# One probability tile for both key blocks, a first piece fed by kinds of parts, and last norms on ScalarE, in a hybrid decoder layer

## The chip, the core and the metric

The kernel runs on one core of one Trainium2 chip. Five engines work in parallel and meet through semaphores: TensorE (PE in the profile; its weight loads are listed apart as PEld), VectorE (DVE), ScalarE (ACT), GpSimd (POOL) and SyncE (SP), which here only issues transfers. Operands lie in SBUF, matmul results in PSUM, inputs and outputs in DRAM. The metric is the device time of one execution in microseconds; lower is better. Before the change it is 973.95, the median of three runs.

## What is computed

One layer over 1024 tokens with 16 learned tokens in front, width 1024, all in float32. Normalised input is projected once into queries, keys, values and two inputs of a recurrence. Eight attention heads (64 wide, two key/value heads) look at a window of 128 keys and at a per-head sink; a gated recurrence with a short convolution runs beside them. Both go through an output projection and a norm onto the residual stream; a feed-forward of width 4096 with squared relu follows.

```python
u = RMSNorm(h)
z = u @ W_in -> [q | k | v | x_rec | y_rec]
...
h += RMSNorm(concat(B_out, A_out) @ W_out)
h += RMSNorm(W2 relu(W1 RMSNorm(h))^2)
...
kk = jnp.concatenate([jnp.pad(kb, blk_pad)[:, :-1], kb], axis=2)
s = jnp.einsum("bnqkgd,bnskd->bnkgqs", qb, kk,
               preferred_element_type=jnp.float32) * scale
...
valid = (diff >= 0) & (diff < WINDOW) & (kpos[:, None, :] >= PAD)
s = jnp.where(valid[None, :, None, None], s, NEG)
m = jnp.maximum(jnp.max(s, axis=-1, keepdims=True), sink)
p = jnp.exp(s - m)
denom = jnp.sum(p, axis=-1, keepdims=True) + jnp.exp(sink - m)
o = jnp.einsum("bnkgqs,bnskd->bnqkgd", (p / denom).astype(v.dtype), vv)
```

Window and block are both 128. So query i of a block may see key i' of its own block where i' <= i, and key i' of the block before where i' > i: of each pair of keys at the same place in the two blocks exactly one is valid.

## The kernel before

**Precision.** Each float32 operand of a large matmul is kept as two parts, a rounded high part and a low part (what the rounding left), and a product is three matmuls: high by high, high by low, low by high (`mm3`, lines 121 to 125). ACT writes the high part, DVE subtracts it from the source to get the low one (`split`, 93 to 100; `split_scaled`, 115).

**Order.** A scheduler lays out each engine's instructions in program order with priorities; `behind` (105) adds an order by hand between two instructions, `lut` (81) keeps ACT's table functions in their written order. Buffers are slots of named pools (`raw`, `ws`, `a`, `b`, `c`, `d`, `e`); a load into a slot waits for the slot's last reader. SP issues most loads, POOL the accumulating stores.

**Start.** x comes in tiles of 128 tokens, with the 16 learned tokens in front. `norm_rows` (197 to 203) squares a tile on ACT, takes the power -0.5 on POOL (`rstd_of`, 155 to 165) and scales on DVE (202). `transposed` (235 to 250) turns the tile by PE and splits it into the two parts of u. This goes by four pieces of tokens (272, 256, 256, 256). For each piece the loop at 345 projects K, V, the first Q pair and the first recurrence input. The weights' parts are made at 277 to 281, ahead of and after the first piece's transposes. `put_k` (300 to 305) writes the high part of K on ACT, its copy into the other half of the partitions on DVE (304) and the low part on DVE (305).

**Attention.** A unit is a pair j of heads (one from each key/value head, h = 0 and 1) and a half of the sequence (four query blocks): 8 units, 16 heads-and-halves. `scores` (432 to 484) makes 128 x 256 scores per query block (previous and own key block), adds the mask and takes the minimum of the negated scores in one DVE instruction (467), exponentiates on ACT, and scales by the reciprocal sum (480). `attend` (486 to 523) turns the probabilities by PE, eight 128 x 128 transposes per head (495), splits them and multiplies by V (506): a key block serves two query blocks, so its matmul is 256 wide, except the first and the last, which are 128. Masks for the general and the first block are made at 365 to 382, V's parts at 409 to 422. Between the units the matmuls of other projections and of the recurrence are put as fill (568 to 600).

**Middle and end.** The recurrence's gates are block-diagonal matrices, built in a zeroed tile (604). Output projection, norm and feed-forward follow. In the feed-forward's last part the four token tiles of the second half and then those of the first are closed one by one: `finish_early` (1120 to 1128), `finish_half` (1132 to 1146), `finish_late` (1148 to 1180). `finish_late` adds both column halves' results, sums squares (1165), takes the power -0.5 on POOL (1173) and combines (1177) with the residual, which was either loaded before or is added by an accumulating store of POOL. `LASTW` (1041) names the slot pools of the last weights.

Of the kernel before, what the change touches and what calls it, by code (L numbers as in the profile page):

```python
# [16 lines left out]
P = 128  # L17
# [20 lines left out]
def hybrid_layer(  # L38
# [76 lines left out]
    def split_scaled(hi, lo, src, scale):  # L115
        nc.scalar.activation(hi, src, AF.Copy, scale=scale)
        nc.vector.scalar_tensor_tensor(
            lo, src, scale, f32(hi), op0=ALU.mult, op1=ALU.subtract
        )

    def mm3(dst, lhs, rhs, start, stop):
        (lh, ll), (rh, rl) = lhs, rhs
        nc.tensor.matmul(dst, lh, rh, start=start, stop=False, skip_group_check=True)  # L123
        nc.tensor.matmul(dst, lh, rl, start=False, stop=False, skip_group_check=True)  # L124
        nc.tensor.matmul(dst, ll, rh, start=False, stop=stop, skip_group_check=True)  # L125
# [29 lines left out]
    def rstd_of(ssq_parts, n=P):  # L155
# [8 lines left out]
        nc.gpsimd.tensor_tensor(rs[:n], ms[:n], half_pow[:n], op=ALU.pow)  # L164
# [32 lines left out]
    def norm_rows(src, n):  # L197
        xn = slot("d", [P, D])
        ssq = small.tile([P, 1], F32, name="ssq", tag="ssq")
        nc.scalar.activation(xn[:n], src, AF.Square, scale=RMS_SC, accum_out=ssq[:n])  # L200
        rs = rstd_of([ssq[:n]], n)
        nc.vector.tensor_scalar(xn[:n], src, rs, None, op0=ALU.mult)
        return xn
# [13 lines left out]

    ALL = [(0, 272), (272, 256), (528, 256), (784, 256)]
    REAL2 = [(16, 512), (528, 512)]

# [5 lines left out]
    nc.vector.tensor_copy(vm.rearrange("p a b -> p (a b)"), zero[:, :256])  # L226
# [8 lines left out]
    def transposed(b, xn):  # L235
        t0, n = ALL[b]
        for kc in range(KC):
# [3 lines left out]
            for s, m in xn:  # L241
                nc.tensor.transpose(
                    pt[:, o : o + m], s[:m, kc * P : (kc + 1) * P], ident[:m, :m]
                )
                o += m
            uh, ul = u[kc]
            split_scaled(
                uh[:, t0 : t0 + n], ul[:, t0 : t0 + n], pt[:, :n],
                g_mix_col[:, kc : kc + 1],
            )  # L250

# [25 lines left out]
    wk = split_w(rk, "b")  # L277
    wv = split_w(rv, "b")
    transposed(0, xn)
    wq = split_w(rq)  # L280
    wx = split_w(rx)
# [7 lines left out]


    khh = [slot("b", [P, T], F32R) for _ in range(2)]
    kl = [slot("b", [P, T], F32R) for _ in range(2)]

    vk = [slot("b", [P, 8, P], F32R) for _ in range(2)]
    HALF = (slice(0, HD), slice(HD, P))
    vt = slot("c", [P, TT])
    for h in range(2):
        nc.gpsimd.memset(f32(kl[h][HALF[1 - h]]), 0.0)

    def put_k(hh, lo, src):  # L300
        for h in range(2):
            r, o = HALF[h], HALF[1 - h]
            nc.scalar.copy(hh[h][r], src[r])
            nc.vector.tensor_copy(hh[h][o], src[r])
            nc.vector.tensor_tensor(lo[h][r], src[r], f32(hh[h][r]), op=ALU.subtract)  # L305

    def sink_k(acc, t0, n):
        o = 0
        if t0 == 0:
            m = slice(0, NMETA)  # L310
            put_k(
                [km[:, 0, m], km[:, 1, m]], [km[:, 2, m], km[:, 3, m]], acc[:, m]
            )
            o = NMETA
        c = slice(t0 + o - NMETA, t0 - NMETA + n)
        put_k(
            [khh[0][:, c], khh[1][:, c]], [kl[0][:, c], kl[1][:, c]], acc[:, o:]
        )

    def sink_v(acc, t0, n):  # L320
        nc.scalar.copy(vt[:, t0 : t0 + n], acc)

    def new_q():
# [3 lines left out]
        def sink_q(acc, t0, n):  # L327
            c = slice(t0 - NMETA, t0 - NMETA + n)
            for h in range(2):
                r, o = HALF[h], HALF[1 - h]  # L330
                split_scaled(q[h][r, c], q[h][o, c], acc[r], HD ** -0.5)
# [10 lines left out]

    q0, sink_q0 = new_q()
    xr0, sink_x0 = new_x("c")
    for b in range(4):
        if b:
            transposed(b, normed(b))
        piece = [ALL[b]]
        project(wk, piece, sink_k)
        project(wv, piece, sink_v)  # L350
        project(wq, piece if b else [(16, 256)], sink_q0)
        project(wx, piece, sink_x0)
# [4 lines left out]
    for c in range(NLRU):  # L357
# [7 lines left out]
    mask = const.tile([P, 256], F32, name="mask")  # L365
    nc.gpsimd.memset(mask, 0.0)
    nc.gpsimd.affine_select(
        out=mask[:, 0:P], in_=mask[:, 0:P], pattern=[[1, P]], compare_op=ALU.is_gt,
        fill=NEG, base=0, channel_multiplier=-1,
    )  # L370
    nc.gpsimd.affine_select(
        out=mask[:, P:256], in_=mask[:, P:256], pattern=[[-1, P]],
        compare_op=ALU.is_ge, fill=NEG, base=0, channel_multiplier=1,
    )
    mask1 = const.tile([P, 256], F32, name="mask1")
    nc.gpsimd.memset(mask1[:, 0:P], NEG)
    nc.gpsimd.memset(mask1[:, 0:NMETA], 0.0)
    nc.gpsimd.affine_select(
        out=mask1[:, 0:NMETA], in_=mask1[:, 0:NMETA], pattern=[[1, NMETA]],
        compare_op=ALU.is_gt, fill=NEG, base=P - NMETA, channel_multiplier=-1,  # L380
    )
    nc.gpsimd.tensor_copy(mask1[:, P:256], mask[:, P:256])
# [30 lines left out]

    pv = bank("o")
    nc.tensor.transpose(pv[:NMETA, :P], vt[:, :NMETA], ident)
    put_v([vm[:NMETA, 0, :], vm[:NMETA, 1, :]], pv[:NMETA, :P])
    for b in range(2):
# [4 lines left out]
        put_v([vk[0][:, 4 * b : 4 * b + 4, :], vk[1][:, 4 * b : 4 * b + 4, :]], pv)  # L422
# [9 lines left out]
    def scores(j, half, q):  # L432
        sn = [slot("c", [P, 4, 257]) for _ in range(2)]
# [3 lines left out]
        for h in range(2):  # L437
            nc.vector.tensor_copy(
                sn[h][:, :, 256], nsink[:, j + 4 * h : j + 4 * h + 1].to_broadcast([P, 4])
            )  # L440
        for bp in range(2):
            for h in range(2):
# [21 lines left out]
                for i in range(2):  # L464
                    b = 4 * half + 2 * bp + i
                    k = 2 * bp + i
                    nc.vector.tensor_tensor_reduce(
                        out=sn[h][:, k, 0:256], in0=sp_[:, i, :],
                        in1=mask1 if b == 0 else mask, scale=-1.0,
                        scalar=nsink[:, j + 4 * h : j + 4 * h + 1],  # L470
                        op0=ALU.add, op1=ALU.min, accum_out=negm[:, h, k : k + 1],
                    )
                    lut(
                        sn[h][:, k, :], sn[h][:, k, :], AF.Exp, scale=-1.0,
                        bias=negm[:, h, k : k + 1], accum_out=den[:, h, k : k + 1],
                    )
        for h in range(2):
            nc.vector.reciprocal(rden[:, h, :], den[:, h, :])
            for k in range(4):
                nc.vector.tensor_scalar(  # L480
                    sn[h][:, k, 0:256], sn[h][:, k, 0:256], rden[:, h, k : k + 1],
                    None, op0=ALU.mult,
                )
        return sn

    def attend(j, half, sn):
        flat = [t_.rearrange("p a b -> p (a b)") for t_ in sn]
        for h in range(2):
            ph, pl = pair("c", [P, 1024])
            for bp in range(2):  # L490
                pt = bank("pt")
                for i in range(2):
                    for s in range(2):
                        o = (2 * i + s) * P
                        nc.tensor.transpose(  # L495
                            pt[:, o : o + P],
                            sn[h][:, 2 * bp + i, s * P : (s + 1) * P], ident,
                        )
                c = slice(512 * bp, 512 * bp + 512)
                split(ph[:, c], pl[:, c], pt)  # L500
            po = bank("o")

            def av(kb, oc, n, pc, first, last):
                v = vm[:, h, :] if kb == 0 else vk[h][:, kb - 1, :]
                for k, p_ in enumerate((ph, pl)):
                    nc.tensor.matmul(  # L506
                        po[:, oc : oc + n], v, p_[:, pc : pc + n],
                        start=first and k == 0, stop=last and k == 1,
                        skip_group_check=True,
                    )  # L510

            kb0 = 4 * half
            av(kb0, 0, P, 0, True, False)
            for i in range(3):
                av(kb0 + 1 + i, i * P, 256, P + 256 * i, False, False)
            av(kb0 + 4, 3 * P, P, 7 * P, False, True)

            r, o = HALF[h], HALF[1 - h]
            part, whole = flat[h][r, 0:512], flat[0][r, 512:1024]
            nc.scalar.copy(part, po[o, :])  # L520
            nc.vector.tensor_tensor(whole, po[r, :], part, op=ALU.add)
        ah, al = at[half][j // 2]
        split(ah[:, j % 2, :], al[:, j % 2, :], flat[0][:, 512:1024])
# [80 lines left out]
    nc.gpsimd.memset(graw, 0.0)  # L604
# [411 lines left out]
    def product_by_parts(acc, w, op):  # L1016
# [25 lines left out]
        ("raw", None), ("e", "raw"), ("b", None), ("b", None), ("raw", "e"), ("b", None),  # L1042
# [43 lines left out]


# [32 lines left out]
    def finish_early(j):  # L1120
        acc = facc["1", j]
        o = slot("a", [P, D])
        ssq = [squares(o[:, c], acc[:, c], n) for n, c in enumerate(COLS)]
        nc.vector.scalar_tensor_tensor(
            o, acc, rstd_of(ssq), gffn_b, op0=ALU.mult, op1=ALU.mult
# [6 lines left out]
    def finish_half(j):  # L1132
# [6 lines left out]
        )  # L1139
        h = None  # L1140
        if j > 1:
            h = slot("d", [P, D])
            nc.sync.dma_start(h, out[j * P : (j + 1) * P, :])
            nc.gpsimd.tensor_scalar(ssq, ssq, EPS, None, op0=ALU.add)
# [137 lines left out]
```

## Time and profile before

| what | value |
| --- | --- |
| median of three runs | 973.95 us (972.76 to 975.39) |
| profiled execution, whole time | 972.95 us |
| its span in the profile | 971.1 us |
| outside the span | 1.85 us |
| mean granted TensorE clock | 0.999 |
| instructions | 12490 |
| first projection matmul starts | 11.18 us |
| 48 matmuls of K and V, first piece, end | 22.42 us |
| last matmul starts | 963.72 us |
| first raw weight load near the end, issue to landing | 907.68 to 916.87 us |

The profile is of one execution. A busy time is the sum over an engine's instructions; a share is of the span. Start to start distances of matmuls are read from the trace's timeline, since matmuls overlap and their ends are modelled. Masked reductions (L467) number 64 and take 0.41 us each, scalings of the probabilities (L480) 64 of 0.285, low parts of the turned probabilities 32 of 0.6.

### The profile page before, as it was taken

The numbers are of one execution on the slowest core, as the hardware profiler recorded it, in microseconds if no ns is written. First come the engines' busy times: TensorE is split into PE (matmuls) and PEld (weight loads), VectorE is DVE, ScalarE is ACT, GpSimd is POOL, SyncE is SP. The second block draws the span as 40 slices with busy tenths as digits, with TensorE's granted clock in tenths as the row PEclk, the third lists the DMA queues.
The fourth block names the chain that finished last, engine by engine and source line by source line (L and its number), as shares of the span: only waits on it lengthen the run. The fifth ranks groups of instructions, "written<-read, shape, count | busy, mean of one in ns | idle before, by whom it ended". The sixth has DMA issues, their size and how long they took to land.

```text
span 971.1 us, 12490 instructions
## 1 busy us (share of the span) xinstructions
PE 953.7 (98%) x4782; PEld 803.0 (83%) x4782; DVE 674.6 (69%) x997; ACT 502.0 (52%) x809; POOL 82.4 (8%) x109
## 2 busy tenths in 40 slices
PE   6999999999999999999999999999999999999997
PEld 6999999888878887888888878888888888888786
DVE  6679997775976686665645465468557676779694
ACT  6646673567844554343555556555433344445350
POOL 4100000000002100000000000000111000003152
PEclk9999999999999999999999999999999999999999
DMA  9002001012234466576522264323678765548923
GB/s 296 23 1 66 23 23 44 23 48 64 84 119 144 159 207 209 173 251 209 198 87 87 97 206 125 114 87 114 172 176 198 186 224 187 184 163 195 223 80 87
DMA packets 88219, 130.13 MB, mean 134 GB/s; under 512 B 13624, under 2 KB 52552, under 8 KB 88160
## 3 DMA queue, kind: packets, MB, share of 16 engines
q1 hardware_dynamic: 79792, 107.33, 33.4%
q0 software_dynamic: 7792, 20.45, 10.1%
q10 hardware_dynamic: 576, 1.57, 0.4%
q8 instruction: 37, 0.61, 0.2%
q14 instruction: 22, 0.18, 0.1%
HBM read 110.46 MB, written 18.87 MB: 133 GB/s over the span
## 4 chain that ended last, share of the span: by engine, by line
PE 89%; DVE 4%; DMA 3%; issue 2%; ACT 1%; POOL 0%; SPq 0%; POOLq 0%; DVEq 0%; ACTq 0%
PE ps_acc L124 11%; PE ps_acc L123 11%; PE ps_acc L125 11%; PE ps_s L125 6%; PE ps_pt L123 6%; PE ps_s L124 6%; PE ps_pt L125 6%; PE ps_s L123 6%; PE ps_pt L124 6%; PE ps_o L124 5%; PE ps_o L123 5%; PE ps_o L125 5%; PE ps_o L506 2%; PE ps_pt L495 1%; DMA raw<-in_w_ff_dram 1%
## 5 line engine op out<-in xcount | busy, mean ns | idle before, releaser
L95 ACT CAST ws<-raw 128x1024 fp32r<-128x1024 f32 (+1 forms) x69 | 70.7, 1024 | 126.6 <-PE ps_o L124 48.8
L98 DVE TENSOR_TENSOR ws<-raw,ws 128x1024 fp32r<-128x1024 f32 (+1 forms) x70 | 83.5, 1194 | 59.6 <-ACT ws L95 59.5
L123 PE MATMUL ps_acc<-a,ws 128*128 128x256 f32 (+2 forms) x272 | 90.5, 333 | 0.6 <-DVE b L305 0.6
L124 PE MATMUL ps_acc<-a,ws 128*128 128x256 f32 (+2 forms) x272 | 89.8, 330 | 0.0
L125 PE MATMUL ps_acc<-a,ws 128*128 128x256 f32 (+2 forms) x272 | 89.4, 329 | 0.0
L98 DVE TENSOR_TENSOR b<-b,b 128x1024 fp32r<-128x1024 f32 (+2 forms) x48 | 57.6, 1201 | 24.7 <-PE ps_o L124 17.1
L95 ACT CAST ws<-e 128x1024 fp32r<-128x1024 f32 x43 | 45.0, 1046 | 55.3 <-PE ps_o L124 28.1
L95 ACT CAST b<-b 128x1024 fp32r<-128x1024 f32 (+2 forms) x48 | 49.4, 1030 | 42.8 <-DVE b L788 40.0
L98 DVE TENSOR_TENSOR ws<-e,ws 128x1024 fp32r<-128x1024 f32 x43 | 52.6, 1222 | 21.6 <-ACT ws L95 21.6
L123 PEld LDWEIGHTS ps_acc<-a,ws 128*128 128x128 f32 x272 | 51.2, 188 | 4.9 <-DVE b L305 0.8
L125 PEld LDWEIGHTS ps_acc<-a,ws 128*128 128x128 f32 x272 | 51.2, 188 | 4.6
L124 PEld LDWEIGHTS ps_acc<-a,ws 128*128 128x128 f32 x272 | 51.2, 188 | 3.9
L164 POOL TENSOR_TENSOR rs<-ms,half_pow 128x1 f32<-128x1 f32 (+1 forms) x31 | 21.3, 692 | 356.5 <-DVE ms L160 355.1
L123 PE MATMUL ps_acc<-ws,b 128*128 128x512 f32 (+1 forms) x120 | 46.3, 386 | 0.4 <-ACT ws L95 0.4
L124 PE MATMUL ps_acc<-ws,b 128*128 128x512 f32 (+1 forms) x120 | 46.5, 388 | 0.2 <-DVE ws L98 0.2
L125 PE MATMUL ps_acc<-ws,b 128*128 128x512 f32 (+1 forms) x120 | 46.2, 385 | 0.0
L123 PE MATMUL ps_pt<-ws,b 128*128 128x512 f32 x112 | 44.1, 394 | 0.0
L124 PE MATMUL ps_pt<-ws,b 128*128 128x512 f32 x112 | 44.1, 394 | 0.0
L125 PE MATMUL ps_pt<-ws,b 128*128 128x512 f32 x112 | 44.0, 393 | 0.0
L123 PE MATMUL ps_s<-ws,b 128*128 128x512 f32 x110 | 43.4, 395 | 0.0
L124 PE MATMUL ps_s<-ws,b 128*128 128x512 f32 x110 | 43.3, 393 | 0.0
L125 PE MATMUL ps_s<-ws,b 128*128 128x512 f32 x110 | 43.3, 393 | 0.0
(381 smaller groups left out, 2690.1 us busy)
## 6 DMA issues: line engine op xcount, KB each, us to landing
raw<-in_w_ff_dram SPq DMA_DIRECT2D x62, 512.0 KB, 4.0
e<-in_w_ff_dram SPq DMA_DIRECT2D x45, 512.0 KB, 3.6
d<-in_w_ff_dram SPq DMA_DIRECT2D x12, 512.0 KB, 3.8
s_dram<-d POOLq DMA_DIRECT2D x12, 512.0 KB, 3.9
raw<-in_w_in_dram SPq DMA_DIRECT2D x9, 512.0 KB, 3.6
c<-in_x_dram SPq DMA_DIRECT2D x8, 512.0 KB, 8.5
d<-in_x_dram SPq DMA_DIRECT2D x8, 512.0 KB, 4.6
out_dram<-raw SPq DMA_DIRECT2D x8, 512.0 KB, 2.6
```

Source lines behind the costliest of these rows:

```text
L95: nc.scalar.copy(hi, src)
L98: low = nc.vector.tensor_tensor(lo, src, f32(hi), op=ALU.subtract).ins
L123: nc.tensor.matmul(dst, lh, rh, start=start, stop=False, skip_group_check=True)
L124: nc.tensor.matmul(dst, lh, rl, start=False, stop=False, skip_group_check=True)
L125: nc.tensor.matmul(dst, ll, rh, start=False, stop=stop, skip_group_check=True)
L164: nc.gpsimd.tensor_tensor(rs[:n], ms[:n], half_pow[:n], op=ALU.pow)
L495: nc.tensor.transpose(pt[:, o : o + P], sn[h][:, 2 * bp + i, s * P : (s + 1) * P], ident,)
L506: nc.tensor.matmul(po[:, oc : oc + n], v, p_[:, pc : pc + n], start=first and k == 0, stop=last and k == 1, skip_group_check=True,)
```

## The change

**Attention.** Scores of both key blocks go into one 128 x 128 tile per query block. The scores come out negated (q is scaled by a negative factor). ACT copies the own block's scores into the tile, DVE overwrites with the previous block's where the key lies above the diagonal (`above`); for the first block a second predicated copy fills the missing keys with a large number (`far`). One DVE reduction takes the minimum over 129 columns (128 and the sink), four exponentials and one normalisation follow, and four transposes per head in place of eight. After the split, POOL makes a second copy of each part in which only the own block's keys are kept and the rest is zero. The product with V is: all entries by V of the previous block, plus the masked copy by the difference of own and previous V. That makes 16 matmuls of 128 columns per head. POOL forms the differences (`vdf`), and V's parts are made from float32 copies in SBUF (`vf`, `vm_f`).

**First piece.** Only wk's high part is made ahead of the first transposes; ACT's and DVE's work is chained by hand; K's and V's matmuls of the first piece run by kinds: high by high for all eight chunks, then high by low, then low by high. The norms of the next two tiles stand between. POOL's clearing of the low parts of K moves to its start. K's copies in the other half of the partitions are made after the fourth piece by POOL transfers. Each later piece's transposes are ordered behind the matmuls of the piece before it; the clearing of `graw` (line 604) is ordered behind POOL's last power.

**Last norms.** The root is taken by ACT and inverted by DVE; ACT's table for it is loaded once ahead of the last part. The tile j = 2 takes the accumulating store as j = 0 and 1 do; j = 3 combines column half by column half. The first of the last weights has its buffer in `b` and not in `raw`.

Counts of instructions, before and after: PE 4782 and 4814 matmuls, DVE 947 and 831, ACT 658 and 673, POOL 107 and 141, SP 222 and 220.

```diff
+    def root_rstd(ssq, bias, n=P):
+        sd = small.tile([P, 1], F32, name="sd", tag="sd")
+        lut(sd[:n], ssq, AF.Sqrt, bias=bias)
+        rs = small.tile([P, 1], F32, name="rs", tag="rs")
+        nc.vector.reciprocal(rs[:n], sd[:n])
         return rs[:n]
...
+    def part(acc, w, piece, k, last=2):
+        t0, n = piece
+        for kc in range(KC):
+            last_mm[0] = nc.tensor.matmul(
+                acc[:, :n], w[k // 2][:, kc, :], u[kc][k % 2][:, t0 : t0 + n],
...
-    wk = split_w(rk, "b")
-    wv = split_w(rv, "b")
+    wk = high_w(rk, "b")
     transposed(0, xn)
-    wq = split_w(rq)
-    wx = split_w(rx)
+    low_w(wk, rk)
+    wv = high_w(rv, "b")
+    low_w(wv, rv)
+    wq = high_w(rq)
+    low_w(wq, rq)
...
-            nc.vector.tensor_copy(hh[h][o], src[r])
...
+            for a, w in zip(acc, (wk, wv)):
+                part(a, w, piece, 0)
+                part(a, w, piece, 1)
+            xn = [(norm_rows(xt[2], P, True), P)]
+            part(acc[0], wk, piece, 2)
+            sink_k(acc[0][:, : piece[1]], *piece)
...
+    for h in range(2):
+        r, o, m = HALF[h], HALF[1 - h], slice(P - NMETA, P)
+        nc.gpsimd.dma_start(f32(khh[h][o]), f32(khh[h][r]))
+        nc.gpsimd.dma_start(f32(km[o, h, m]), f32(km[r, h, m]))
...
-                for i in range(2):
-                    b = 4 * half + 2 * bp + i
-                    k = 2 * bp + i
-                    nc.vector.tensor_tensor_reduce(
-                        out=sn[h][:, k, 0:256], in0=sp_[:, i, :],
-                        in1=mask1 if b == 0 else mask, scale=-1.0,
...
+                s_ = sn[:, h, 2 * bp : 2 * bp + 2, 0:P]
+                nc.scalar.copy(s_, sp_[:, :, P:256])
+                nc.vector.copy_predicated(
+                    s_, above_i.rearrange("p (a b) -> p a b", a=1).to_broadcast([P, 2, P]),
+                    sp_[:, :, 0:P],
+                )
...
+            nc.vector.tensor_reduce(
+                negm[:, h, :], sn[:, h], axis=mybir.AxisListType.X, op=ALU.min
+            )
...
+            nc.vector.tensor_tensor(
+                sn[:, h, :, 0:P], sn[:, h, :, 0:P],
+                rden[:, h, :].to_broadcast([P, 4, P]), op=ALU.mult,
+            )
...
+            for i in range(4):
+                nc.tensor.transpose(pt[:, i * P : (i + 1) * P], sn[:, h, i, 0:P], ident)
+            pt = pt.rearrange("p (a b) -> p a b", a=4)
+            split(ph[:, 0], pl[:, 0], pt)
+            for p_ in (ph, pl):
+                nc.gpsimd.affine_select(
+                    out=p_[:, 1], in_=f32(p_[:, 0]), pattern=[[0, 4], [1, P]],
+                    compare_op=ALU.is_ge, fill=0.0, base=0, channel_multiplier=-1,
                 )
...
+            for s in range(2):
+                for i in range(4):
+                    b = 4 * half + i
+                    v = vd[h][:, b, :] if s else vk[h][:, b - 1, :] if b else vm[:, h, :]
+                    for k, p_ in enumerate((ph, pl)):
+                        nc.tensor.matmul(
+                            po[:, i * P : (i + 1) * P], v, p_[:, s, i, :],
...
-            av(kb0, 0, P, 0, True, False)
-            for i in range(3):
-                av(kb0 + 1 + i, i * P, 256, P + 256 * i, False, False)
-            av(kb0 + 4, 3 * P, P, 7 * P, False, True)
...
-    nc.gpsimd.memset(graw, 0.0)
+    behind(last_pow[0], nc.gpsimd.memset(graw, 0.0).ins)
...
-        ("raw", None), ("e", "raw"), ("b", None), ("b", None), ("raw", "e"), ("b", None),
+        ("b", None), ("e", "raw"), ("b", None), ("b", None), ("raw", "e"), ("b", None),
...
-            if j < 2:
+            if j < 3:
                 w_low[0] = nc.vector.scalar_tensor_tensor(
-                    o, acc, rstd_of([squares(o[:, c], acc[:, c], 0), ssq]), gffn_b,
+                    o, acc, root_rstd(squares(o[:, c], acc[:, c], 0), ssq), gffn_b,
...
+            if k == 1:
+                rs = root_rstd(ssq, 0.0)
+            w_low[0] = combine(o[:, c], acc[:, c], gffn_b[:, c], ALU.mult).name
...
-        nc.gpsimd.tensor_tensor(rs, ssq, half_pow, op=ALU.pow)
```

## The prediction, made before the changed kernel was run

> **What bounds the kernel now.** I read the totals first, then the chain that ended last, then both ends and two middle stretches by engine, then starts of single matmuls.
>
> ```profile
> span 971.1 us, 12490 instructions
> PE 953.7 (98%) x4782; PEld 803.0 (83%) x4782; DVE 674.6 (69%) x997; ACT 502.0 (52%) x809; POOL 82.4 (8%) x109
> PE 89%; DVE 4%; DMA 3%; issue 2%; ACT 1%; POOL 0%; SPq 0%; POOLq 0%; DVEq 0%; ACTq 0%
> ```
>
> PE is busy 98% of the span and holds 89% of the chain. So an edit pays only if it takes matmul time away, or shortens the two ends or one of PE's few stalls.
>
> ```profile
> 0.00:10.00 10.00, 2.68 (x14) 2.07 (x14) 4.61 (x9) 6.26 (x9) 6.36 (x22) 1.00 0.84 254
> 10.00:20.00 10.00, 9.32 (x42) 8.67 (x43) 8.61 (x14) 8.76 (x17) 3.65 (x7) 1.00 1.05 379
> 80.00:100.00 20.00, 20.00 (x147) 18.81 (x147) 19.65 (x54) 14.63 (x36) 0.00 (x0) 1.00 0.09 27
> 260.00:275.00 15.00, 14.59 (x64) 11.50 (x63) 15.00 (x16) 9.33 (x14) 0.00 (x0) 1.00 0.17 64
> 940.00:971.10 31.10, 24.00 (x132) 20.46 (x130) 18.33 (x28) 3.84 (x7) 11.87 (x7) 0.95 0.29 68
> ```
>
> Columns: stretch, length, busy time of PE, weight loads, DVE, ACT, POOL (counts), granted clock, DMA share, GB/s. PE lacks 7.3 us in the first ten, about 7 at the end (the last matmul starts at 963.72), and 0.4 in the stretch with the stall at 271.82. At 80 to 100 DVE is nearly full, yet PE never waits. Matmul starts after 20 us show four more gaps: 28.09 (0.79, on DVE's L305), 365.08 (0.84), 918.05 and 919.31 (0.57 and 0.34).
>
> ```profile
> 13.81 0.43 PE L123 MATMUL ps_acc<-a,b 128*128 128x272 f32 x1
> 14.04 0.43 PE L124 MATMUL ps_acc<-a,b 128*128 128x272 f32 x1
> ...
> 20.25 0.28 PE L123 MATMUL ps_acc<-a,b 128*128 128x272 f32 x1
> 20.37 0.29 PE L124 MATMUL ps_acc<-a,b 128*128 128x272 f32 x1
> ...
> 88.11 0.22 PE L447 MATMUL ps_s<-km,b 128*128 128x128 f32 x1
> 88.17 0.28 PE L451 MATMUL ps_s<-km,b 128*128 128x128 f32 x1
> 88.28 0.27 PE L447 MATMUL ps_s<-b,b 128*128 128x128 f32 x1
> 88.39 0.28 PE L451 MATMUL ps_s<-b,b 128*128 128x128 f32 x1
> ...
> 116.97 1.00 PE ps_o L506 x9
> 117.97 0.90 PE ps_pt L495 x8
> ```
>
> Start to start, 272 columns cost 0.227 us until about 19.2 and 0.125 after (the granted clock reads 1.00 throughout, so the slow start is read from spacing). 128 columns cost 0.059 once and then 0.11: in an unbroken run the weight load sets the pace, not the columns. A head's av matmuls (4 of 128 columns, 6 of 256) take 1.00, its 8 transposes 0.90.
>
> **Attention: +3.2, and +0.8 of waiting.** Per head and half (16 of these) the transposes go from 8 to 4, and the av matmuls from 10 to 16, all 128 wide: the same columns, more weight loads. I priced the order of PE's instructions at 0.451 ns a column (0.231 for 512) but at least 0.1105 from start to start where loads follow each other. Before: 16.2 for av + 14.1 for transposes = 30.3. After: 27.2 + 6.3 = 33.5, since 15 or 16 av matmuls stand unbroken and only in four-transpose groups next to wide matmuls is a load hidden. Bounds: 0.111 is a measured row, so hardly above +3.2; the 0.059 row gives the lower one (rival A). I take +3.2.
>
> DVE loses 64 masked reductions (0.41), 64 scalings (0.285) and 16 low parts (0.6), 54 us; it gains 32 predicated copies over both blocks (plus 8 small), 16 reductions over 4x129, 16 normalisations and the V pieces. None of these forms is in the trace; by rows of 0.41 to 0.69 for up to 512 elements they are 30 to 45. ACT loses 16 casts, gains 32 copies of scores. Both hide under PE, as DVE does at 80 to 100: zero. Uncovered, each lost microsecond of DVE there would count.
>
> The new wait is transposes, ACT's cast (0.5), DVE's low part (0.6), two masked copies on POOL, av. POOL's 128x128 select rows are 0.28 to 0.47, its 128x1024 memset 0.96: 0.5 to 1.9 for 128x512, I take 1.0. The path is 2.7 to 4.9; by PE's new order 4.5 to 7.5 us of fill matmuls stand between. Behind a late av wait that unit's fills, and with them everything on PE. But POOL can be held up:
>
> ```profile
> 939.65 7.24 POOL L1144 TENSOR_SCALAR late<-late 128x1 f32<-128x1 f32 x1 [1.95 <-ACT a L1137]
> 965.29 0.99 POOL L1173 TENSOR_TENSOR rs<-part,half_pow 128x1 f32<-128x1 f32 x1 [2.87 <-DVE part L1165]
> ```
>
> One column takes 7.24 here and ends as DVE runs out of work; alone such a step takes 0.5. Bounds 0 to +6.4 (rival C); I take +0.8, nearer to nothing, as DVE gets shorter here. The Trainium skill, SBUF — State Buffer, on the shared port pair, has DVE and GpSimd arbitrate by an exclusive lock that lasts a whole instruction; the 7.24 row agrees, and by it the selects wait for whole DVE instructions (its result is rival C).
>
> **First piece: -3.0.** Before, DVE scales xt[1] from 8.40 in 1.52 (0.76 for xt[0], which runs beside no 2.4 us POOL memset), then makes wk's and wv's low parts from 9.85 in 2.34, so the low part of u starts at 12.11. ACT casts both weights first, until 9.5. The 48 k and v matmuls end at 22.42, the first projection having started at 11.18. After, POOL's memsets come first, only wk's high part precedes u's, and the parts need hi·hi first, then u's low, then w's. By rows (ACT u-hi 0.375, DVE u-lo 0.41 to 0.49, each 8 times, from about 9.65) PE is fed one chunk per 0.4 and ends the 48 between 19.6 and 20.7: -1.7 to -2.8. The 0.79 stall goes, as the duplicate copies of L304 leave DVE, and a little goes at the next piece, whose norms are prepared earlier. Bounds -1.5 and -4.5. What could be late instead: x[2]'s and x[3]'s norms on ACT and DVE between the parts, of 0.75 each; the hi·lo parts cover them.
>
> K's second halves go by two 64x1024 and two 64x16 POOL DMAs after piece 3. 512 KB stores land in 3.9 after issue (section 6 of the page), these are half of that; with four issues of about 1 us the last is there 7 to 8 us after the last sink, and piece 3's q and x matmuls (48 of 256 columns at 0.118 = 5.7), the transposes of V and the first fills lie between: zero, +3 if late (rival D). Through the wait put on the memset of graw SP's loads behind it wait for POOL's last power; its raw slots only come free near 72 us, so nothing is late.
>
> **Middle: -0.5.** At 271.82 PE waits 0.56 for the recurrence's products; the new order puts 1.4 us more matmul time ahead of that use: -0.6 to 0.
> **Last weights: -0.7.**
>
> ```profile
> 907.68 9.19 DMA raw<-in_w_ff_dram
> ```
>
> This load (normally 4.0) starts at 907.68, behind POOL's accumulating store, and PE waits 0.9 at its end. In a b buffer it is no longer behind that raw slot. If that buffer is freed no sooner, the wait stays or grows: -0.9 to +1.
> **Last norms: -0.65.** Part ready 965.14, power until 966.28, final combine 966.31 (1.15). After: a root on ACT (small ACT rows 0.17 to 0.25), a reciprocal on DVE (0.17), hops 0.1: 0.5 instead of 1.15. -0.3 to -0.9. The stores after it stay. The extra table load (1.28) falls where ACT has 5.7 us idle (260 to 275): zero; without that cover it costs its length once. The removed load and two stores of j=2 lie ahead of the end's bound.
>
> **Sum:** 3.2 + 0.8 - 3.0 - 0.5 - 0.7 - 0.65 = -0.85. The span goes from 971.1 to 970.25; 1.85 lies outside it (972.95 - 971.1): 972.1. The median of the runs stands 1.0 over that execution (973.95): **973.1**. About 0.3%, 2.9 us, is what a measurement of this kernel can tell from no change, so the limits are 971.0 and 976.9.
>
> **Rivals.** A, narrow matmuls are cheap: the two of a pair (high and low p) share their v, so only each second waits for its load: (0.059 + 0.111)/2 = 0.085. Av 256 x 0.085 = 21.8, + 6.3 = 28.1, -2.2 instead of +3.2: **967.7**. For it speaks the 0.059 row; against it that the profile counts a weight load for each matmul (x4782 both) and that steady runs in the trace are at 0.11. In the Trainium skill, TensorE: Matmul & The Clock Gate, section Back-to-back issue gap, N=128 sustains about 81 ns a matmul; by it 320 of them would be 25.9, an estimate, which this trace's 0.11 does not bear out.
> B, the start gives more: the step from 0.227 to 0.125 comes after a stretch of steady matmuls, which starts sooner; a microsecond sooner saves 4 cold matmuls' excess, and no new wait in attention: 973.1 - 1.6 - 0.8 = **970.7**. Against: the steady stream before starts at 12.66, and the parts now begin with a trickle.
> C, the slow side: masked copies on POOL wait behind DVE's instructions with two SBUF sources. Two waits of 0.6 (half of L98's 1.2) on the path of about 4 make 5.2 against the shortest cover of 4.5; this decides once the path passes 4.5. At 0.4 a head over 16 heads it is +6.4 for +0.8: **978.7**. For it: the 7.24 row and a nearly full DVE at 80 to 100; against: DVE loses work there.
> D, K's copies late: the first scores wait 3: **976.1**.
> That the attention does not get narrower is excluded: PE's instruction counts (4782 to 4814) show it.
>
> **Chances.** Forecast 0.38 (own range 971 to 976; 0.04 below 971.0, 0.02 above 976.9), A 0.15 (all faster), B 0.18 (0.12 faster), C 0.22 (0.21 slower), D 0.07 (0.03 slower). Faster 0.04 + 0.15 + 0.12 = 0.31; slower 0.02 + 0.21 + 0.03 = 0.26; same 0.43. Below 967.0 lies about 0.07 (A with loads hidden still more often), above 979.5 about 0.1 (C at full price): the range is 967.0 to 979.5.
>
> **What will show it.** Attention: av runs of 16 at 0.11 (A: 0.085), no gaps on PE ahead of av; C: gaps whose releaser is POOL's select. Start: the 48th k and v matmul before 20.7, no stall at 28. Middle and last weights: gaps at 271 and 918 gone. End: 0.5 from the last part to the final combine. I am wrong if PE's columns do not set the pace in the middle, or if POOL's copies appear in the chain.

## The result, and the profile after

Over 13 runs of each, the median is 976.11 us (974.67 to 978.27) after the change and 974.45 (972.31 to 975.52) before: a ratio of 1.0022, 95% interval 1.0012 to 1.0032. The change makes the kernel about 2 us slower. The forecast was 973.1, a gain of 0.85: the range holds the time, the sign is wrong. One execution in the sections below, of the kernel with norms and slot alone, took 2443.79 where its other ten took 972.76 to 974.79; it is left out of that kernel's median and ratio.

The profiled execution took 976.60, its span is 974.9; the two profiled executions lie 3.65 apart, more than the medians. Its totals, and the stretches that were shown of before (columns as there; the last one is as far from the end):

```profile
span 974.9 us, 12513 instructions
...
PE 956.3 (98%) x4814; PEld 804.2 (82%) x4814; DVE 652.9 (67%) x834; ACT 504.2 (52%) x850; POOL 95.0 (10%) x153
...
PE 82%; DVE 6%; DMA 5%; ACT 3%; issue 2%; POOL 0%; SPq 0%; DVEq 0%; ACTq 0%; POOLq 0%
```

```profile
0.00:10.00 10.00, 2.63 (x13) 2.08 (x14) 3.65 (x7) 5.43 (x8) 6.10 (x20) 1.00 0.80 228
10.00:20.00 10.00, 9.89 (x61) 9.08 (x60) 7.61 (x12) 7.65 (x17) 1.57 (x2) 1.00 1.11 335
80.00:100.00 20.00, 19.44 (x164) 18.98 (x163) 13.96 (x28) 13.54 (x48) 2.75 (x6) 1.00 0.09 27
260.00:275.00 15.00, 14.11 (x61) 10.83 (x60) 14.32 (x15) 10.31 (x16) 0.00 (x0) 1.00 0.12 36
944.00:974.90 30.90, 22.96 (x126) 19.65 (x124) 14.17 (x24) 3.26 (x10) 2.67 (x3) 0.92 0.38 69
```

The first 20 us hold 74 matmuls where they held 56: the start works. In 80 to 100 DVE falls from 19.65 to 13.96, yet PE loses 0.56, which it did not before. In 260 to 275 PE loses 0.89 where it lost 0.41. The last matmul starts at 966.68 (before: 963.72), and 8.2 us follow it where 7.3 did. So of the 3.8 us between the two spans 3.0 had arisen when PE ended and 0.9 arose behind it.

The steady rate of the narrow matmuls is read from the chain that ended last, where runs of them stand as one piece:

```profile
89.69 1.62 PE ps_o L632 x15
...
106.51 1.73 PE ps_o L632 x16
```

That is 0.108 each for av matmuls of 128 columns, where 0.111 was taken. POOL's selects, by groups (busy time, mean ns, then idle time and what ended it):

```profile
L619 POOL TENSOR_SCALAR_AFFINE_SELECT c<-c 128x512 fp32r<-128x512 f32 x32 | 23.3, 728 | 106.7 <-ACT c L95 100.7 <-DVE c L98 5.1 <-POOL c L619 0.8
```

They take 0.73 and not 1.0, and nearly all of POOL's idle time before them ends when the split part that they read is there.

### The profile page after: what moved, and what is told of

It reads as the page before. It is cut to its first block, busy times and chain, and to the rows that moved or that the text cites. A ratio compares the mean times of both kernels' runs of the same rounds, so it can differ in the third digit from the quotient of the medians.

```text
span 974.9 us, 12513 instructions
## 1 busy us (share of the span) xinstructions
PE 956.3 (98%) x4814; PEld 804.2 (82%) x4814; DVE 652.9 (67%) x834; ACT 504.2 (52%) x850; POOL 95.0 (10%) x153
## 3 DMA queue, kind: packets, MB, share of 16 engines
q0 software_dynamic: 8160, 21.51, 10.7%
## 4 chain that ended last, share of the span: by engine, by line
PE 82%; DVE 6%; DMA 5%; ACT 3%; issue 2%; POOL 0%; SPq 0%; DVEq 0%; ACTq 0%; POOLq 0%
PE ps_acc L124 9%; PE ps_acc L125 9%; PE ps_acc L126 9%; PE ps_pt L124 6%; PE ps_pt L125 6%; PE ps_pt L126 6%; PE ps_o L124 5%; PE ps_o L126 5%; PE ps_o L125 5%; PE ps_s L126 5%; PE ps_s L124 5%; PE ps_s L125 5%; PE ps_o L632 3%; DMA d<-in_w_ff_dram 2%; DMA s_dram<-d 1%
## 5 line engine op out<-in xcount | busy, mean ns | idle before, releaser
L124 PE MATMUL ps_acc<-a,ws 128*128 128x256 f32 (+2 forms) x256 | 85.7, 335 | 0.6 <-ACT d L421 0.5
L125 PE MATMUL ps_acc<-a,ws 128*128 128x256 f32 (+2 forms) x256 | 85.1, 333 | 0.0
L126 PE MATMUL ps_acc<-a,ws 128*128 128x256 f32 (+2 forms) x256 | 85.1, 332 | 0.0
L95 ACT CAST ws<-e 128x1024 fp32r<-128x1024 f32 x41 | 42.8, 1045 | 66.8 <-PE ps_o L125 33.8
L98 DVE TENSOR_TENSOR ws<-e,ws 128x1024 fp32r<-128x1024 f32 x41 | 50.1, 1222 | 23.4 <-ACT ws L95 23.4
L124 PEld LDWEIGHTS ps_acc<-a,ws 128*128 128x128 f32 x256 | 48.2, 188 | 5.3 <-ACT d L421 0.8
L126 PEld LDWEIGHTS ps_acc<-a,ws 128*128 128x128 f32 x256 | 48.2, 188 | 4.4
L125 PEld LDWEIGHTS ps_acc<-a,ws 128*128 128x128 f32 x256 | 48.2, 188 | 4.0
L124 PE MATMUL ps_o<-ws,b 128*128 128x512 f32 (+1 forms) x108 | 41.4, 384 | 0.0
```

The lines of the kernel that those rows point to most:

```text
L95: nc.scalar.copy(hi, src)
L98: low = nc.vector.tensor_tensor(lo, src, f32(hi), op=ALU.subtract).ins
L126: last_mm[0] = nc.tensor.matmul(dst, ll, rh, start=False, stop=stop, skip_group_check=True).ins.name
```

## The experiments

Each time is a median; each ratio is to the kernel before, run on the same chip in the same rounds (its medians there: 973.69 to 974.15), with its 95% interval. "Slot" is the first of the last weights' buffer (raw or b).

| kernel | us | ratio (interval) |
| --- | --- | --- |
| all parts (the change) | 976.11 | 1.0022 (1.0012 to 1.0032) |
| attention alone, changed order of K and Q | 980.08 | 1.0061 (1.0046 to 1.0077) |
| the same, slot in b | 983.59 | 1.0096 (1.0078 to 1.0113) |
| start alone | 978.52 | 1.0044 (1.0028 to 1.0059) |
| norms and slot alone | 973.61 | 0.9996 (0.9985 to 1.0006) |
| norms and slot, changed order of K and Q | 978.10 | 1.0036 (1.0022 to 1.0051) |
| that order alone | 979.25 | 1.0052 (1.0032 to 1.0072) |
| attention, norms and slot | 978.75 | 1.0051 (1.0033 to 1.0068) |
| the same, changed order of K and Q | 978.15 | 1.0044 (1.0032 to 1.0056) |
| all but attention | 977.89 | 1.0039 (1.0024 to 1.0054) |
| all but the slot | 975.81 | 1.0021 (1.0011 to 1.0032) |
| all, j=2 from a loaded residual | 974.80 | 1.0006 (0.9995 to 1.0018) |
| all, root's table loaded later | 975.43 | 1.0014 (1.0003 to 1.0025) |
| all, both of these | 974.37 | 0.9995 (0.9984 to 1.0007) |
| all, wide av with two selects | 971.98 | 0.9980 (0.9972 to 0.9989) |
| the same, j=2 from a loaded residual | 971.09 | 0.9972 (0.9962 to 0.9982) |
| the same, root's table later too | 969.02 | 0.9941 (0.9921 to 0.9961) |

### Attention alone, the start undone, and wide av

The first kernel keeps the changed attention and takes back the rest (K's and Q's parts stay in the changed order: ACT's for both heads, then DVE's, where the old order goes head by head). The second takes back the first piece only.

> The attention of the changed kernel with the first piece (K's second copies by DVE among it), the last norms and the last weights' slot of the kernel before. Theory (weight loads of 128-wide av matmuls): PE's instruction order costs 3.05 us more than before and the first unit waits about 0.9, so about 974.45 + 4 = 978.4. Rival (POOL's masked copies come late): gaps on PE ahead of av in many heads, 980 or more. Rival (narrow matmuls cost nothing and the loss lies in the other parts): 974.5 or less.

> The changed kernel with the first piece of the kernel before (K's second copies by DVE, weights' parts all made first, K's low parts cleared later on POOL). Theory (the new start is worth 1.9 us and nothing gives it back): 976.1 + 1.9 = 978.0, and the matmuls of attention are later by as much. Rival (the gain is lost again at the first unit, whose scores wait for K, Q or the softmax): 976.1 to 977, with no wait at the first unit.

980.08 and 978.15. The second is as the theory had it: with the new attention the new start is worth 2.0 us. The first is higher than expected, but not through the selects: its largest stall is 2.28 us at 926, on a last weight, and a stretch at half speed behind it. So it does not price attention cleanly.

> The changed kernel with two masked copies of each part of the turned probabilities in place of one (POOL: 64 selects of 128x512 and not 32), so that a key block serves two query blocks again and a head's av matmuls are 10 (4 of 128 columns, 6 of 256), not 16 of 128; the differences of V are not made. Theory (weight loads set the pace of 128-wide matmuls): counting PE's order with 0.1105 us between loads gives 10.7 us less than for the changed kernel, so about 965.5. Rival (POOL's selects are on the path): two more selects of 0.73 ahead of av in each head, 16 x 1.5 = 24 us given back where no cover is left, 976 to 989, with gaps on PE released by the select.

```diff
-            split(ph[:, 0], pl[:, 0], pt)
+            split(ph[:, :, 0, :], pl[:, :, 0, :], pt)
             for p_ in (ph, pl):
...
+                nc.gpsimd.affine_select(
+                    out=p_[:, :, 0, :], in_=f32(p_[:, :, 0, :]), pattern=[[0, 4], [-1, P]],
+                    compare_op=ALU.is_gt, fill=0.0, base=0, channel_multiplier=1,
+                )
...
+            av(kb0, 0, P, 0, True, False)
+            for i in range(3):
+                av(kb0 + 1 + i, i * P, 256, P + 256 * i, False, False)
+            av(kb0 + 4, 3 * P, P, 7 * P, False, True)
```

971.98: 4.1 less than the change, where 10.7 was counted. The mechanism holds: the hundred-and-first 512-wide matmul starts 9.5 us earlier (156.41, not 165.91), although POOL now makes 64 selects. PE waits for a select once, 0.38 at 146.27 (POOL by time, then DVE, then PE):

```profile
143.03 0.63 POOL L612 TENSOR_SCALAR_AFFINE_SELECT c<-c 128x512 fp32r<-128x512 f32 x1
143.73 2.48 POOL L616 TENSOR_SCALAR_AFFINE_SELECT c<-c 128x512 fp32r<-128x512 f32 x1
...
143.83 1.28 DVE L658 SCALAR_TENSOR_TENSOR d<-d,prm,d 128x1038 f32<-128x1038 f32 x1
...
146.27 0.33 PE L629 MATMUL ps_o<-c,vm 128*128 128x128 f32 x1 [0.38 <-POOL c L616]
```

The second select takes 2.48 beside DVE instructions that read two tiles of SBUF, the first 0.63: rival C's mechanism is there, at a small part of its price. A longer wait, 1.2 at 149.15, ends with DVE's normalisation (L594) behind the exponentials. The lead over the changed kernel, taken at the same 512-wide matmul, is 9.3 at 255 and 5.9 at 284 (the changed kernel's times): the recurrence's chain of table functions on ACT ends only 4.1 earlier (257.86, not 261.94), and PE waits 2.94 for a cast behind it and the root's table.

```profile
260.87 0.50 PE L124 MATMUL ps_pt<-a,b 128*128 128x512 f32 x1 [2.94 <-ACT b L95]
261.21 0.39 PE L125 MATMUL ps_pt<-a,b 128*128 128x512 f32 x1
...
262.87 0.63 PE L125 MATMUL ps_o<-a,b 128*128 128x512 f32 x1
263.29 0.63 PE L124 MATMUL ps_acc<-a,b 128*128 128x512 f32 x1
```

Starts lie 0.23 apart after the wait, then 0.42 (262.87 to 263.29) for seven matmuls: the wait costs 1.4 us more than its length.

### The end: j=2, the root's table

```diff
-        if j > 2:
+        if j > 1:
             h = slot("d", [P, D])
             nc.sync.dma_start(h, out[j * P : (j + 1) * P, :])
...
-            if j < 3:
+            if j < 2:
```

> The changed kernel, with tile j=2 finished from a residual loaded ahead and plain stores. Theory (the accumulating store of j=2 is still running when the last two stores start and makes them land 1.2 us later): last stores land as in the kernel before, about 4.0 us after the final combine starts and not 5.9, and 976.1 - 1.2 = 974.9. Rival (DVE's combine for j=2 is what delays the last part): the final combine earlier, the stores as slow as now, 975.5 to 976.1.

974.80, as forecast from the accumulating store. In the changed kernel the end reads (POOL, DVE, ACT, by time):

```profile
967.17 0.88 POOL L1286 DMA_DIRECT2D out_dram<-a  x1 [3.73 <-issue]
...
968.92 1.41 DVE L1300 SCALAR_TENSOR_TENSOR a<-a,rs,d 128x512 f32<-128x512 f32 x2
...
970.36 0.35 ACTq L1303 DMA_DIRECT2D out_dram<-a  x1
```

POOL issues j=2's accumulating store of 512 KB at 967.17, 2.5 us ahead of the first of the two last stores; the three accumulating stores at this kernel's end land 5.5 after issue in the median, so it is still in flight when those start. The last combine in the kernel before and in the one with j=2 from a loaded residual:

```profile
966.31 1.41 DVE L1177 SCALAR_TENSOR_TENSOR a<-a,rs,d 128x512 f32<-128x512 f32 x2 [0.44 <-POOL rs L1173]
...
968.26 1.41 DVE L1300 SCALAR_TENSOR_TENSOR a<-a,rs,d 128x512 f32<-128x512 f32 x2
```

From its start to the end of the span it takes 5.97 in the changed kernel (974.89 - 968.92), 4.75 before (971.06 - 966.31) and 4.87 with j=2 from a loaded residual (973.13 - 968.26).

The root's table: what stands ahead of PE's wait at 273.71 in the changed kernel, from the chain of waits, and then the same DVE instruction with its idle time.

```profile
261.94 1.28 ACT L82
263.23 0.01 issue
263.24 0.02 ACT root L82
263.26 0.09 issue
263.35 1.04 ACT a L95
264.39 0.02 issue
264.41 1.08 DVE a L98
...
264.41 1.23 DVE L98 TENSOR_TENSOR a<-d,a 128x1024 fp32r<-128x1024 f32 x1 [0.68 <-ACT a L95]
```

The first line is the added table load. The cast of W_out starts behind it, and DVE, whose queue holds the low part next and the recurrence's scans after it, has stood idle for 0.68 when the cast ends.

```diff
-    load_root()
     done = set()
...
+    load_root()
     LAST = 3
...
-        lut(root, eps_col, AF.Sqrt)
+        behind(last_hi[0], lut(root, eps_col, AF.Sqrt))
```

(`last_hi` is the last high part that ACT has written.)

> The changed kernel, with the table of the root loaded after the feed-forward's casts have begun and not right behind the recurrence's last gelu. Theory (the load of 1.28 and the first root of 0.20 stand ahead of casts of W_out on ACT, and PE waits for them at 270 to 274): the two waits there (0.40 and 0.81) fall to 0.56 in all or less, 976.1 - 0.7 = 975.4. Rival (these waits come from DVE's scans, whatever ACT does): no change there, 976.1.

975.43: the two waits (0.40 and 0.81) become one of 0.54. By the times alone this step is not told from noise (intervals 1.0003 to 1.0025 and 1.0012 to 1.0032); the waits show it. Both mended:

> The changed kernel with the two mended steps alone: j=2 from a loaded residual, the root's table held back. Theory (the two are independent): 976.1 - 1.3 - 0.7 = 974.1, level with the kernel before. Rival (the earlier PE only waits longer for the last stores or weights): 974.8 to 975.4.

974.37, level with the kernel before. These two steps are thus worth the whole loss. The same two on the wide form, in turn (in the first the table load still stood ahead of the casts, since ACT's order put it there; in the second a `behind` holds it back):

> As the run before, and in the last part tile j=2 is finished with a residual loaded ahead and plain stores as in the kernel before, and the root's table is loaded ahead of the last four tiles and not ahead of the output projection. Theory (the accumulating store of j=2 holds up the last stores by 1.2 us; the table load delays casts that PE waits for by 0.6): 1.8 us under the run before, about 963.7. Rival (the end is set by the last norm's chain and the stores in any order; the wait near 273 comes from DVE's scans alone): the same as the run before within 0.5.

> The wide av matmuls with two masked copies, j=2 finished from a residual loaded ahead, and the root's table now held back on ACT until the feed-forward's casts (in the earlier run of this kind it still stood ahead of the casts of W_out). Theory (the wait of 3.08 us near 260 ends with ACT: table load 1.28, root 0.20, then the casts): the wait falls to 1.6 and part of the 1.4 us of half-speed matmuls behind it goes, so 971.1 - 1.5 to 2.9 = 968.2 to 969.6. Rival (DVE's scans end no earlier): 971.

971.09: 0.9 less, by the end; the wait near 260 stays (3.09 from start to start), as the load was not moved. Then 969.02: the wait falls to 1.58 and no matmul behind it is slow. This form beats both kernels, by 0.59% (0.39 to 0.79) against the one before.

### What attention is worth without the start

These kernels take back parts of the change's own diff: the start and the last norms (first), attention (second), all but the start (third), attention and start (fourth); all four keep the changed order of K and Q.

> The changed attention and the last weights' slot of the changed kernel, with the first piece and the last norms of the kernel before. Theory (attention costs 3.05 us of PE time and 0.6 at the first unit, and the slot in b takes away the wait near 918, 0.9 in the kernel before): 973.8 + 2.8 = 976.6, and no wait near 926, where the run with attention alone had 4.2. Rival (that wait comes with the shift of attention, not with the raw slot): still a wait of 2 us or more there, and 979 to 980.

> The changed kernel with the attention of the kernel before (two key blocks side by side, eight transposes, ten av matmuls, two masks, K's 16 learned keys at the tile's start). Theory (attention is what costs): 3.4 us less by the count of PE's order and 0.9 less wait at the first unit, so 976.1 - 4.3 = 971.8. Rival (the other parts cost, attention is neutral, since DVE's longer work comes back as waits): 974 to 976.

> The kernel before with the changed first piece alone (K's second copies by transfer among it). Theory (the gain at the start is lost again in the attention of the kernel before, whose DVE work has no slack): PE ahead by about 2 until 80, waits of 2 us or more for DVE near the end of attention, and 974.0 or more. Rival (the start's gain goes through to the end): 972.1.

> The kernel before with the changed last norms and last weights' slot alone. Theory: the wait near 918 goes (0.9 and a short slow stretch, -1.2), the stores of j=2 add 0.9 at the end, the table load adds up to 0.6: 974.0 to 974.4. With the run that has all but the changed start (978.15) this gives attention's own price without the new start, some 4 us. Rival (the last norms cost by themselves): 976 or more, and attention's price is then 2 or less.

983.59, 977.89, 978.52 and 978.10. The third is as its theory had it; the other three are 3.7 us or more above theirs. In the first, POOL's queue explains it (POOL, then DVE, by time):

```profile
909.52 1.22 POOL L1147 DMA_DIRECT2D b<-in_w_ff_dram  x1 [9.39 <-issue]
910.27 1.05 POOL L169 TENSOR_TENSOR rs<-ms,half_pow 128x1 f32<-128x1 f32 x1
...
911.36 1.28 DVE L1215 SCALAR_TENSOR_TENSOR a<-b,rs,a 128x1024 f32<-128x1024 f32 x1 [8.94 <-POOL rs L169]
912.56 1.22 DVE L98 TENSOR_TENSOR ws<-e,ws 128x1024 fp32r<-128x1024 f32 x1
```

An accumulating load of the last weights stands at the head of POOL's queue for 9.39 before it is issued (the profile names no releaser); the power of a norm is queued behind it, DVE waits 8.94 for that power, the next weight's low part waits behind DVE's combine, and PE waits 4.6; with the stretch at half speed behind it that is most of the 7.0 above the theory. With the norms on ACT the power is gone from POOL's queue. The other three share a wait near 155. Since they also share the order of K's and Q's parts, that was tried next:

> The kernel before with one change alone: the high parts of K and Q for both heads are written on ACT first, then DVE's parts for both, in place of head after head. Theory (DVE's chain through the attention of the kernel before has no slack, and this order makes the scheduler lay it out later): a wait of 2 us and a stretch at half speed near 155, as in the run with the norms alone and in the run with the start alone, 977.5 to 978.5. Rival (that wait comes from the start and the norms): 974.1, no wait.

```diff
             for h in range(2):
+                r = HALF[h]
+                nc.scalar.activation(q[h][r, c], acc[r], AF.Copy, scale=HD ** -0.5)
+            for h in range(2):
                 r, o = HALF[h], HALF[1 - h]
-                split_scaled(q[h][r, c], q[h][o, c], acc[r], HD ** -0.5)
+                nc.vector.scalar_tensor_tensor(
...
```

(K's parts likewise; there the parts of the 16 learned keys also come behind those of the other keys.) 979.25 from this alone. In its chain of waits, and in the stretch:

```profile
151.78 1.22 DVE d L621
153.00 0.02 issue
153.03 0.39 ACT d L420
153.42 0.04 issue
153.47 0.44 PE ps_acc L124
153.91 0.21 PE ps_acc L125
```

```profile
140.00:160.00 20.00, 17.92 (x138) 17.54 (x137) 15.54 (x36) 9.69 (x26) 0.00 (x0) 0.91 0.10 27
```

PE waits 2.21 for ACT to empty a PSUM bank into a buffer of pool d, and that buffer for DVE's convolution (L621), which the scheduler's new order put between the parts of the last softmax. The kernel before has PE full there (20.00). The granted clock is 0.91, from the slow matmuls after the wait. Why the scheduler answers so strongly to so small a change was not pursued. In the next two kernels K's and Q's parts are in the old order:

> The kernel before with the changed last norms and last weights' slot alone; the order in which K's and Q's parts are written from PSUM is that of the kernel before too (in the earlier run of this name it was the changed one). Theory (norms: +0.9 at the end by the store of j=2, up to +0.6 by the table load, -1.2 by the last weights): 974.0 to 974.5 and no wait near 155. Rival (the last norms cost by themselves): 977 or more again.

> The changed kernel with the whole start of the kernel before, the order of K's and Q's parts among it. Theory (the changed attention leaves DVE slack, so that this order does not matter there, and its price is PE's 3 us and the first unit's 0.6): 978 as in the run with the changed order, no wait near 155. Rival (the order matters as much with the changed attention): 976 or less, or 980 or more.

With K's and Q's parts in the old order the norms and the slot are worth nothing (973.61), and attention on top of them costs 5.1 (978.75). The time of the new attention hardly depends on the order (978.75 and 978.15), so in the changed order, which costs the old attention 4.5, it costs nothing on top of norms and slot (978.15 and 978.10).

```diff
     LASTW = [
-        ("b", None), ("e", "raw"), ("b", None), ("b", None), ("raw", "e"), ("b", None),
+        ("raw", None), ("e", "raw"), ("b", None), ("b", None), ("raw", "e"), ("b", None),
```

> The changed kernel with the first of the last weights in its raw slot as in the kernel before. Theory (with the norms off POOL's queue the slot in b saves the wait near 918): a wait of 0.9 to 4 us near 920, so 977 to 980. Rival (the slot matters only beside the norms on POOL): no wait, 976.1.

975.81: the theory fell. Two waits of 0.34 and 0.35 come in (at 922.57 and 945.52), the time stays within the runs' scatter. The slot matters much only beside norms on POOL (980.08 and 983.59).

## Why the prediction was wrong

By adding parts in the old order of K and Q: norms, slot and middle 0 (973.61 against 973.69, within the interval; the wait near 918 that goes pays for the end and the table load), attention +5.1, the start -2.6 (976.11 - 978.75).

The two profiled executions tell the same by stages. Each row ends at a matmul that both kernels run, and says how much the changed kernel lost there; the last projection matmul of the second piece (41.38, before 44.20) and a 512-wide matmul behind attention (244.63, 242.50) end the first two, PE's last matmul the fifth.

| stage | forecast | profiles |
| --- | --- | --- |
| start | -3.0 | -2.8 |
| attention | +4.0 | +5.0 |
| middle, to 284.22 (before 281.41) | -0.5 | +0.7 |
| feed-forward, to 872.18 (before 867.60) | 0 | +1.8 |
| last weights, to 966.68 (before 963.72) | -0.7 | -1.6 |
| end | -0.65 | +0.9 |
| sum | -0.85 | +3.8 |

The medians are 1.7 us apart and not 3.8, since the profiled execution of the kernel before lies 1.5 below its median and the changed one's 0.5 above. So the rows hold some 2 us that belong to these two executions; which rows, one profile of each can't tell.

- **Attention, +3.2 and +0.8: right in kind, a little small.** 0.108 a matmul agrees with the count. The waiting came, 0.68 at 85.54 in the changed kernel (below) and 1.23 and 0.74 at 74 and 91 without the new start; none of these ends with POOL's select. They end with ACT emptying a bank, behind the exponentials in the first and behind a weight's cast in the second, and with the predicated copy in the third. Rival C falls: twice as many selects cost 0.38. Rival A falls too: the loads set the pace, and replacing a head's 16 narrow matmuls by 10, 6 of them wide, gained 9.5.

```profile
85.20 0.30 ACT d L421
85.50 0.04 issue
85.54 0.39 PE ps_acc L124
```

- **DVE's edits at zero: incomplete.** DVE's busy time falls by 21.7 us over the span. With the old attention the order of K and Q that comes with the new start costs 4.5 to 5.6 us, with the new one nothing: in the old attention the chain that ends near 155 is mostly DVE's. So start and norms with the old attention give 977.89. A new start with the old order and the old attention was not tried.
- **First piece, -3.0: right.** The 48 matmuls end at 20 and not at 22.4; the wait at 28.09 is gone, one of 0.69 at 21.45 came. It is worth 2.8 at its own end and 2.0 to 2.6 in the runs. Rival B's step is there: 272 columns take 0.125 from 14.4 on, before from 19.4. But the gain that B adds is not. Rival D falls: PE's longest wait between 30 and 80 is 0.28.
- **Middle, -0.5: wrong sign.** The failed step is "The extra table load (1.28) falls where ACT has 5.7 us idle (260 to 275): zero". The idle time lies behind the casts, the load ahead of them. Waits went from 0.56 to 1.21; moving the load behind the casts gave 0.7.
- **Feed-forward, put at nothing: +1.8.** The forecast has no term between the middle and the last weights, since no line of that stage was edited. But the same 2,500 matmuls of 512 columns take 587.97 where they took 586.19. Here are the starts of the first of them and of the next behind the last, in the kernel before and then in the changed one:

```profile
281.41 0.39 PE L125 MATMUL ps_acc<-a,b 128*128 128x512 f32 x1
...
867.60 0.40 PE L123 MATMUL ps_acc<-ws,b 128*128 128x512 f32 x1
...
284.22 0.40 PE L126 MATMUL ps_acc<-a,b 128*128 128x512 f32 x1
...
872.18 0.40 PE L124 MATMUL ps_acc<-ws,b 128*128 128x512 f32 x1
```

  About half of it is the distance of the matmuls (last section), the rest small waits. The three kernels with the old order of K and Q take 586.0 to 586.2 there, all others 587.0 to 591.1: the loss comes with the changed order. Why stays open.
- **Last weights, -0.7: the wait went, not by the slot alone.** With norms and slot moved no matmul behind 918 waits. With the norms on ACT but the raw slot 0.34 and 0.35 stay; with the slot in b but the norms on POOL 4.6 comes.
- **Last norms, -0.65: wrong sign.** From PE's end to the last combine 1.96 us pass, 2.31 before: a gain of 0.35, as a combine of 0.42 now stands ahead of the reciprocal. The failed step is "The removed load and two stores of j=2 lie ahead of the end's bound": true of those, but the accumulating store that replaces them was not priced. It costs 1.1 to 1.3, and with it the end is 0.9 later.

Against the forecast the two failed steps cost 1.15 (middle) and 1.55 (end): -0.85 + 1.15 + 1.55 = +1.85, and moving both back brings the kernel level with the one before. That +1.85 comes so near the measured +2.15 (0.0022 x 974) is luck in part: the feed-forward's loss and attention's excess are in no term of it, and the last weights gave more than forecast.

## What to carry to other kernels

When a transfer is replaced, price the one that takes its place and look at what it overlaps at the end, not only at what is saved. A table load or any edit costed at nothing must be placed in its queue: idle time in the same stretch is no cover if it lies behind the work that others wait for. And where an engine off the chain is nearly full, parts of a change do not add: price them on top of each other, in the order in which one makes room for the next. A stage in which no line was edited is no sure zero either: compare the two traces there too.

## What the runs showed of the hardware

After waits of PE of 2.2 to 4.7 us (eight in these kernels, from start to start) matmuls run at about half rate for 3.0 to 3.5 us, in all but attention for 5.2; 512 columns then take 0.427 in place of 0.231. This begins at once or up to 1.6 us later. A wait of 1.58 had no such stretch. The granted clock shows it: 0.91 in the row above, 0.50 from 262.3 to 265.6 in the wide form. Such a wait thus costs 1.4 to 1.9 us on top of its length, in all but attention some 2.4. The Trainium skill, TensorE: Matmul & The Clock Gate, section What's actually happening, has the clock halved after at least one idle window of some 3.4 us; the half rate agrees, but here 2.2 us of waiting were enough.

Between 400 and 900 us, where all these kernels run the same feed-forward, the mean distance of 512-wide matmuls (distances under 0.3 us) is 230.95 ns in the kernel before, with norms and slot alone and with attention, norms and slot; 231.4 in the changed kernel and those made from it by the two mends; 231.95 in all three wide ones; the rest lie between 231.4 and 231.8. Over some 2,160 matmuls that is 1 to 2 us. The three at 230.95 are those with the old order of K's and Q's parts, and three pairs differ in that order alone (the kernel before; norms and slot; attention, norms and slot): the changed order has 0.5 to 0.65 ns more in each. What it changes for the matmuls there stays open.
